# A mixer with a two-level mixture of experts: group places counted one tile later, counts on GpSimd, and other PSUM banks for the sums, the turns and the first down products

## The chip, the cores and the metric

The kernel runs on one core of one Trainium2 chip. The metric is the time of one launch on the device in microseconds; of several runs the median is taken. The engines of the core are named as the profile names them: PE (matmuls; PEld is its weight load), DVE (VectorE), ACT (ScalarE), POOL (GpSimd) and SP (SyncE, which here only issues DMAs). Matmuls write to PSUM, which has eight banks of 512 f32 columns; PE reads its operands from SBUF.

## What is computed

One layer on 1024 tokens of width 1024: a mixer (two kinds of gated linear attention), an output product, a norm, then 64 experts in 8 groups. Each token picks one group, and in it two experts; the experts' outputs are added with gates, and a second norm ends the layer.

```python
h = hybrid_mixer(x, w_in, w_a2, b_a, lb_all, norm_h, norm_g, w_out)
x = layer_norm(DEEPNORM_ALPHA * x + h, ln1_g, ln1_b)
# hierarchical_moe
p_group = softmax(xf @ w_group_router);  p_top_group, g_idx = top_k(p_group, 1)
e_logits = (xf @ w_expert_router)[the group's 8]
p_top, e_local = top_k(softmax(e_logits), 2)
gates = p_top_group * p_top / sum(p_top)
expert_id = g_idx * 8 + e_local
...
h = silu(xb @ w_gate[e]) * (xb @ w_up[e]);  yb = h @ w_down[e]
y = sum over a token's two experts of gate * yb
x = layer_norm(DEEPNORM_ALPHA * x + y, ln2_g, ln2_b)
```

## The kernel before

**Stages.** The mixer's projections and attention run first, to 421 us of the profile. Then comes the output product with the first norm and the router, tile by tile (a tile is 128 tokens, `NT` = 8 tiles). From about 562 us on the experts run in 32 pairs (`pairs`). The weights of all 64 experts, 402 MB, go through SBUF once, in 192 units of 2 MB: per pair two gate units, two up units, two down units. A few units are loaded ahead into the pools `w1` and `w2` (four buffers each) and two single buffers `w3u`. Every later unit takes the buffer of an earlier one, so SP issues its load only when PE has done the last product that reads the earlier one (`load_after`, `load_unit`, L793 and L800). SP issues its loads in program order.

**Router (`router`, L818 on).** For each tile DVE finds the group and the two experts from the logits `lg`, makes the one-hot rows `oh12` and from them `m`, 80 columns: 64 for the experts and 16 (`NE:NM`) for the groups, of which each is split into two classes, c = 0 and 1. A token's places among those of its expert and of its group and class are counts of the tokens ahead of it. `msum` is the running sum of `m` over the tiles before, and `msb` its copy in bf16.

**Places (`ranks`, L871 on).** For tile t two bf16 products add up in one bank `R` (tile name `lp`): `oneb` by `msb` gives the counts of all tiles before (L878), `trib` by `m` those of the tokens ahead in the tile (L879). DVE then reads `R` (`jk`, with the rank as its sum: L908 for the experts, L893 for the group), makes the one-hot `so` and `soc` of the ranks, and `tables` (L930) adds products of them into the bank `tabp`, from which come, for every slot of an expert, token number and gate (`tokf`, `gcol`) and, for every row of a group, its token (`rtok`, `gidx`). The pool of `lp` has one bank, and the logits of most tiles (L1024) use it too.

**Order.** In the loop over the tiles (L1089 on) tile t's output product `w_out`, its norm `norm1`, the places of tile t - 2, and the logits and router of tile t - 1 stand side by side; the order on each engine is set by the tile framework's scheduler, but for a few orders written by hand. In the last tile the places of tiles 6 and 7 follow each other, the table's part for the first expert pair (`sidx`) goes first, and then the rows of the first pair are gathered from `x1d` in DRAM (L1162).

**PSUM at the change of stages.** In the router stage `ps_h` (name `hp`) has banks 0 to 3, `ps_xt` 4 and 5, `ps_l` 6, `ps_t` (`tabp`) 7. In the experts' stage `ps_g` (`gu`) has 0 and 1, `ps_x` (`tp`, turns of x) 2 and 3, `ps_c` (`cp`, the sums) 4 to 7.

**Pairs (L1364 on).** First eight spreads bring the norms' constants, lying along partitions, to all rows (`spread`, L1353, four products of 128 columns each, which a DVE copy L1355 takes to SBUF): two in `gu` banks, four in `cp` banks ahead of pair 0, two in `cp` banks behind its up products. Then for each pair: the gate products (L1404, u = 0) and up products (u = 2) of two experts, 64 rows each; silu on ACT (L1410), the product with the up half on DVE (L1417); the turn of the next pair's rows (L1185 from the gathered rows for pairs 0 and 1; later L1191, products with a 0/1 matrix `pick` out of the group's rows, which `split_rows` has split in three bf16 `parts`); the turn of the hidden rows (L1207); the down products (L1361) into two banks `yps`; and their scaling into `y` by ACT (L1215) and DVE (L1216). The outputs of pair p - 1 are added to the group's rows by products with `adds` between the gate and up products of pair p (`add_rows`, L1322). For pair 0 the scaling comes behind both down products (L1452), since `y` lies where the last weights of pair 0 were. PE's order within `pairs` is the program's; that of the other engines is the scheduler's. The splitting of group 0's rows (L1294 to L1297, pair 1 in the program) is on ACT and DVE, that of later groups on ACT and GpSimd.

Of the kernel before, what the change touches and what calls it, by code (L numbers as in the profile page):

```python
# [10 lines left out]
F32 = mybir.dt.float32  # L11
# [10 lines left out]
NT = T // 128  # L22
# [37 lines left out]
def mixer_moe_kernel(ctx: ExitStack, tc: tile.TileContext, x_in, xT_in, wf_in, wv_in, wvg_in, wa2_in,  # L60
# [757 lines left out]
    def router(t):  # L818
# [18 lines left out]
        m = sp2.tile([128, NM], BF, name="m", bufs=3)  # L837
        msb = sp2.tile([128, NM], BF, name="msb", bufs=3)
        V.tensor_copy(msb, msum)
# [4 lines left out]
        V.scalar_tensor_tensor(mc_[:, :, 0], og, 0.0, mc_[:, :, 1], op0=OP.is_equal, op1=OP.subtract)  # L844
        count = lambda: V.tensor_tensor(msum, msum, m, OP.add)
# [24 lines left out]

    def ranks(t, E=V):  # L871

        m, msb = mt.pop(t)
        R = ps_l.tile([128, NM], F32, name="lp")
        own = t == NT - 1

        def counts(cs):
            PE.matmul(R[:, cs], oneb, msb[:, cs], start=True, stop=False)  # L878
            PE.matmul(R[:, cs], trib, m[:, cs], start=False, stop=True)  # L879
# [5 lines left out]
        def row_of():  # L885

            rhc = sp2.tile([128, 2 * NG], F32, name="rhc", bufs=1)
            if own:
                counts(slice(NE, NM))
            G.tensor_tensor(rhc, m[:, NE:NM], number.to_broadcast([128, 2 * NG]), OP.mult)  # L890
            jk = sp2.tile([128, NE], BF, name="jk")
            rc = sp2.tile([128, 1], F32, name="rc")
            o = V.scalar_tensor_tensor(jk[:, 0:2 * NG], m[:, NE:NM], 1.0, R[:, NE:NM], op0=OP.mult, op1=OP.mult,  # L893
                                       accum_out=rc)
            soc = sp2.tile([128, 128], F32, name="soc", bufs=1)
            V.tensor_tensor(soc, rowrank, rc.to_broadcast([128, 128]), OP.is_equal)
            rowst[t] = soc, rhc
            return o
# [19 lines left out]
        if own:  # L918
            return row_of
        row_of()  # L920
# [9 lines left out]
    def tables(t):  # L930

        so, rhs = rst.pop(t)
        row = PE.matmul(tabp[:, NE:NM], *rowst.pop(t), start=(t == 0), stop=False)
        for j in range(2):
            for b in range(2):
                o = PE.matmul(tabp[64 * b:64 * b + 64, 0:NE], so[:, j], rhs[:, j, b].rearrange("p k a -> p (k a)"),
                              start=False, stop=False)
                order(o, row, "the first product opens the bank")
# [112 lines left out]
    slots = sp2.tile([128, CAP], F32, name="slots", bufs=1)  # L1051
# [3 lines left out]
    expert = sp2.tile([128, NE], F32, name="expert", bufs=1)  # L1055
# [64 lines left out]
    for i, o in enumerate(ranks(t - 1, G)):  # L1120
# [10 lines left out]
    order(row_of(), first, "the rows that are to be fetched go first")  # L1131
# [6 lines left out]
    PE.matmul(gt[:, 32:32 + 2 * NG], *rowst.pop(t), start=True, stop=True)  # L1138
# [12 lines left out]
    ps_g = mp.enter_context(tc.tile_pool(name="ps_g", bufs=2, space=PSUM))  # L1151
    ps_x = mp.enter_context(tc.tile_pool(name="ps_x", bufs=2, space=PSUM))
    ps_c = mp.enter_context(tc.tile_pool(name="ps_c", bufs=4, space=PSUM))
# [58 lines left out]
    def scaled(yps, n, gate_col, yh, yl):  # L1212
# [3 lines left out]
        V.scalar_tensor_tensor(yl[:, ns], yps[n], gate_col, yh[:, ns], op0=OP.mult, op1=OP.subtract)  # L1216
# [72 lines left out]
    def split_rows(g, c, E):  # L1289
# [5 lines left out]
        E.tensor_tensor(rest, x, b0, OP.subtract)  # L1295
# [68 lines left out]
    def pairs():  # L1364

        nonlocal ring, home, parts
# [4 lines left out]
        for p in range(npair):  # L1371
# [54 lines left out]
            yps = [ps_g.tile([128, 512], F32, name="gu") for _ in range(2)]  # L1426
# [244 lines left out]
```

## Time and profile before

| | before |
|---|---|
| median of 3 runs | 1517.71 us (1516.21 to 1518.36) |
| the profiled execution | 1518.87 us, of which the span is 1517.1 |
| PE busy | 1443.5 us (95%) |
| DVE / ACT / POOL busy | 620.6 / 489.2 / 225.8 us (41 / 32 / 15%) |
| moved by DMA | 445.48 MB, mean 294 GB/s over the span |
| mean granted clock of PE | 0.990 |

The shares are means over stages with different limits: the mixer moves little (18 to 50 GB/s in most of its slices), the experts' stage moves 427 to 430 GB/s in most of its slices while PE is also 90% busy or more. The chain of waits that ended last has only two pieces, both at the very end on POOL, and says nothing of the rest. So the tables by stage and the timeline are what to read. One execution was profiled, and PE's half clock comes and goes in stretches of it; the granted clock stands in each row of the tables by stage.

### The profile page before, as it was taken

How to read it: one execution, taken by the hardware profiler on the slowest of the kernel's cores; microseconds unless marked ns; L12 is line 12 of the kernel's file. 1: busy time of each engine (PE TensorE's matmuls, PEld its weight loads, DVE VectorE, ACT ScalarE, POOL GpSimd, SP SyncE). 2: the span in 40 equal slices, each digit the busy share in tenths (PEclk: the TensorE clock that was granted, in tenths of full speed). 3: DMA queues.
4: the chain of work that ended last, by engine and by line, in shares of the span. 5: the costliest groups of instructions: out<-in, count | busy, mean ns of one | idle time of the engine just before them, and what ended most of it. 6: DMA issues, size and time to landing. Idle time of an engine off the chain costs nothing. (4 is left out here: it accounts for less than half of the span.)

```text
span 1517.1 us, 24694 instructions
## 1 busy us (share of the span) xinstructions
PE 1443.5 (95%) x10365; PEld 841.9 (55%) x10365; DVE 620.6 (41%) x1446; ACT 489.2 (32%) x961; POOL 225.8 (15%) x172
## 2 busy tenths in 40 slices
PE   9999999999999898999999999999999999999996
PEld 7888788887888773433433443444444344444432
DVE  6786673948545864142132132033033124114113
ACT  6656554457423323221321221222222221231120
POOL 0000001000012212140140140130130131032000
PEclk9999999999999979999999999999999999999999
DMA  5111111101284257999999999999999999999994
GB/s 182 50 36 43 30 43 29 41 18 45 91 346 168 112 197 279 416 429 428 429 429 427 430 429 427 429 430 426 428 429 427 429 430 427 429 429 427 427 424 202
DMA packets 58292, 445.48 MB, mean 294 GB/s; under 512 B 8916, under 2 KB 17364, under 8 KB 32576
## 3 DMA queue, kind: packets, MB, share of 16 engines
q1 hardware_dynamic: 51184, 430.00, 68.4%
q0 software_dynamic: 4896, 8.84, 1.6%
q10 hardware_dynamic: 2096, 5.01, 0.9%
q8 instruction: 82, 1.34, 0.4%
q14 instruction: 34, 0.28, 0.1%
HBM read 440.24 MB, written 12.58 MB: 298 GB/s over the span
## 5 line engine op out<-in xcount | busy, mean ns | idle before, releaser
L1404 PE MATMUL gu<-w1u,VOA 128*64 128x512 f32 x1024 | 248.1, 598 | 12.1 <-DMA w1u<-in_wu_dram 7.9
L1404 PE MATMUL gu<-w2u,VOA 128*64 128x512 f32 x992 | 239.3, 599 | 8.0 <-DVE y L1216 4.2
L1179 ACT ACTIVATE VOA<-tp,cols 128x128 f32<-128x128 f32 x256 | 96.2, 457 | 353.0 <-PE tp L1191 328.2
L1404 PEld LDWEIGHTS gu<-w1u,VOA 128*64 128x64 f32 x1024 | 83.3, 138 | 166.3 <-issue 131.1
L1404 PEld LDWEIGHTS gu<-w2u,VOA 128*64 128x64 f32 x992 | 88.0, 137 | 145.2 <-issue 108.4
L170 PE MATMUL pp<-xl,wh 128*128 128x512 f32 x416 | 164.8, 396 | 0.0
L170 PE MATMUL pp<-xh,wh 128*128 128x512 f32 x416 | 163.5, 393 | 0.6 <-ACT vt L223 0.6
L170 PE MATMUL pp<-xh,wl 128*128 128x512 f32 x416 | 163.2, 392 | 0.0
L1216 DVE SCALAR_TENSOR_TENSOR y<-gu,gcol,y 128x512 fp32r<-128x512 f32 x62 | 46.4, 750 | 242.7 <-ACT y L1215 242.5
L1361 PE MATMUL gu<-w2u,hT 128*64 128x512 f32 x512 | 117.4, 597 | 12.4 <-ACT VOA L1179 11.6
L1361 PE MATMUL gu<-w1u,hT 128*64 128x512 f32 x480 | 111.1, 598 | 13.4 <-ACT VOA L1179 12.5
L1191 PEld LDWEIGHTS <-parts 128*128 128x128 bf16 x1248 | 69.9, 98 | 48.8 <-issue 48.8
L1215 ACT ACTIVATE y<-gu,gcol 128x512 fp32r<-128x512 f32 x62 | 42.4, 686 | 142.8 <-PE gu L1361 142.8
L1417 DVE TENSOR_TENSOR sg<-sg,gu 128x512 f32<-128x512 f32 x32 | 22.0, 687 | 162.1 <-PE gu L1404 162.1
L170 PEld LDWEIGHTS pp<-xh,wh 128*128 128x128 f32 x416 | 78.1, 188 | 18.0 <-ACT vt L223 1.0
L170 PEld LDWEIGHTS pp<-xl,wh 128*128 128x128 f32 x416 | 78.1, 188 | 16.1 <-issue 0.2
L170 PEld LDWEIGHTS pp<-xh,wl 128*128 128x128 f32 x416 | 78.2, 188 | 15.5
L1410 ACT ACTIVATE sg<-gu 128x512 f32<-128x512 f32 x31 | 18.6, 599 | 195.0 <-PE gu L1404 195.0
L1191 PE MATMUL tp<-pick,parts 128*128 128x128 bf16 x1248 | 80.1, 220 | 0.8 <-DVE hT L1209 0.8
L1361 PEld LDWEIGHTS gu<-w2u,hT 128*64 128x64 f32 x512 | 40.8, 136 | 71.6 <-issue 51.1
L1361 PEld LDWEIGHTS gu<-w1u,hT 128*64 128x64 f32 x480 | 37.7, 136 | 64.8 <-issue 45.6
L1311 DVE TENSOR_SCALAR adds<-grow,tokf 128x256 fp32r<-128x256 f32 x31 | 19.0, 614 | 115.8 <-PE cp L1322 115.8
(343 smaller groups left out, 1961.7 us busy)
## 6 DMA issues: line engine op xcount, KB each, us to landing
w1u<-in_wg_dram SPq DMA_DIRECT2D x30, 2048.0 KB, 25.8
w1u<-in_wu_dram SPq DMA_DIRECT2D x30, 2048.0 KB, 29.0
w2u<-in_wg_dram SPq DMA_DIRECT2D x30, 2048.0 KB, 27.2
w2u<-in_wu_dram SPq DMA_DIRECT2D x30, 2048.0 KB, 29.8
w1u<-in_wd_dram SPq DMA_DIRECT2D x30, 2048.0 KB, 29.2
w2u<-in_wd_dram SPq DMA_DIRECT2D x28, 2048.0 KB, 27.8
wr<-in_wf_dram SPq DMA_DIRECT2D x36, 256.0 KB, 2.8
w1u<-in_wg_dram SPq DMA_DIRECT2D x8, 1024.0 KB, 21.4
```

The costliest lines, as they stand in the source:

```text
L170: PE.matmul(ps, w[:, k], x_[:, k, ts], start=(k == 0 and j == 0), stop=(k == KT - 1 and j == len(terms) - 1))
L1179: S.activation(xt[:, c], tp[:, i], AF.Identity, bias=cols[:, 42 + c:43 + c], scale=cols[:, 34 + c:35 + c])
L1191: PE.matmul(o, part[:, c], m, start=(i == 0), stop=(i == len(ms) - 1))
L1215: S.mul(yh[:, ns], yps[n], gate_col)
L1216: V.scalar_tensor_tensor(yl[:, ns], yps[n], gate_col, yh[:, ns], op0=OP.mult, op1=OP.subtract)
L1311: V.tensor_scalar(m, grow[0], tokf[:, p:p + 1], None, op0=OP.is_equal)
L1361: PE.matmul(yps[n][64 * b:64 * b + 64], hT[:, c, 64 * b:64 * b + 64], utile[6 * p + 4 + b][:, c, n * 512:(n + 1) * 512], start=(c == 0), s ...
L1404: PE.matmul(dst[64 * b:64 * b + 64], xt[:, c, 64 * b:64 * b + 64], utile[6 * p + u + b][:, c], start=(c == 0), stop=(c == KT - 1))
L1410: silu = S.activation(sg, gp, AF.Silu)
L1417: V.tensor_tensor(sg, sg, up, OP.mult)
```

## The change

It has these parts.

1. *Counts on GpSimd.* The copy `msb` and the running add into `msum` move from DVE to GpSimd (but for the last tile's add).
2. *Group places one tile later.* `R` of tile t holds the expert counts of tile t (64 columns) and the group counts of tile t - 1 (16 columns), as separate products. `row_of` becomes a function of its own, and makes the group row of tile t - 1; the last tile's group counts get a bank of their own, `lastR`, from `ps_h`. The first product that opens the bank `tabp` is now one of the expert products, without an order by hand.
3. *Types and forms.* `slots` and `expert` are bf16 instead of f32, and one `scalar_tensor_tensor` becomes a `tensor_tensor` with the same result on 0 and 1.
4. *Banks.* `ps_c` is opened ahead of `ps_x`: `cp` has banks 2 to 5, `tp` 6 and 7.
5. *The first pair's down products* go into two `cp` banks instead of the `gu` banks, and the subtractions that split group 0's rows stand behind the scaling of pair 0's outputs on DVE.

```diff
@@ router
-        m = sp2.tile([128, NM], BF, name="m", bufs=3)
-        msb = sp2.tile([128, NM], BF, name="msb", bufs=3)
-        V.tensor_copy(msb, msum)
+        m = sp2.tile([128, NM], BF, name="m", bufs=4)
+        msb = sp2.tile([128, NM], BF, name="msb", bufs=4)
+        G.tensor_copy(msb, msum)
...
-        V.scalar_tensor_tensor(mc_[:, :, 0], og, 0.0, mc_[:, :, 1], op0=OP.is_equal, op1=OP.subtract)
-        count = lambda: V.tensor_tensor(msum, msum, m, OP.add)
+        V.tensor_tensor(mc_[:, :, 0], og, mc_[:, :, 1], OP.is_equal)
+        count = lambda: (V if t == NT - 1 else G).tensor_tensor(msum, msum, m, OP.add)
@@ row_of, now outside ranks
+    def row_of(t, R):
+        m = mt.pop(t)[0]
+        rhc = sp2.tile([128, 2 * NG], F32, name="rhc", bufs=2)
+        G.tensor_tensor(rhc, m[:, NE:NM], cst[:, C_TOK + t:C_TOK + t + 1].to_broadcast([128, 2 * NG]), OP.mult)
...
+        o = V.scalar_tensor_tensor(jk[:, 0:2 * NG], m[:, NE:NM], 1.0, R[:, NE:NM], op0=OP.mult, op1=OP.mult,
+                                   accum_out=rc)
+        soc = sp2.tile([128, 128], F32, name="soc", bufs=1)
+        V.tensor_tensor(soc, rowrank, rc.to_broadcast([128, 128]), OP.is_equal)
+        rowst[t] = soc, rhc
+        return [o]
@@ ranks
-        def counts(cs):
-            PE.matmul(R[:, cs], oneb, msb[:, cs], start=True, stop=False)
-            PE.matmul(R[:, cs], trib, m[:, cs], start=False, stop=True)
-
-        counts(slice(0, NE if own else NM))
+        sums = [(k, u, cs, w_) for u, cs in ((t, slice(0, NE)), (t - 1, slice(NE, NM))) if u >= 0
+                for k, w_ in ((1, oneb), (0, trib))]
+        for i, (k, u, cs, w_) in enumerate(sums):
+            PE.matmul(R[:, cs], w_, mt[u][k][:, cs], start=(i == 0), stop=(i == len(sums) - 1))
...
-        if own:
-            return row_of
-        row_of()
+        if t:
+            ops += row_of(t - 1, R)
@@ tables
-        row = PE.matmul(tabp[:, NE:NM], *rowst.pop(t), start=(t == 0), stop=False)
...
+                PE.matmul(tabp[64 * b:64 * b + 64, 0:NE], so[:, j], rhs[:, j, b].rearrange("p k a -> p (k a)"),
+                          start=(t == 0 and j == 0), stop=False)
+        if t:
+            PE.matmul(tabp[:, NE:NM], *rowst.pop(t - 1), start=False, stop=False)
@@ behind the loop over the tiles
-    slots = sp2.tile([128, CAP], F32, name="slots", bufs=1)
+    slots = sp2.tile([128, CAP], BF, name="slots", bufs=1)
-    expert = sp2.tile([128, NE], F32, name="expert", bufs=1)
+    expert = sp2.tile([128, NE], BF, name="expert", bufs=1)
...
-    row_of = ranks(t)
+    late = ranks(t)[2:]
...
-    order(row_of(), first, "the rows that are to be fetched go first")
+    lastR = ps_h.tile([128, 512], F32, name="hp")
+    for k, w_ in ((1, oneb), (0, trib)):
+        PE.matmul(lastR[:, NE:NM], w_, mt[t][k][:, NE:NM], start=(k == 1), stop=(k == 0))
+    for o in late + row_of(t, lastR):
+        order(o, first, "the rows that are to be fetched go first")
...
-    PE.matmul(gt[:, 32:32 + 2 * NG], *rowst.pop(t), start=True, stop=True)
+    for u in (t - 1, t):
+        PE.matmul(gt[:, 32:32 + 2 * NG], *rowst.pop(u), start=(u < t), stop=(u == t))
@@ pools of the experts' stage
-    ps_x = mp.enter_context(tc.tile_pool(name="ps_x", bufs=2, space=PSUM))
     ps_c = mp.enter_context(tc.tile_pool(name="ps_c", bufs=4, space=PSUM))
+    ps_x = mp.enter_context(tc.tile_pool(name="ps_x", bufs=2, space=PSUM))
@@ split_rows
-        E.tensor_tensor(rest, x, b0, OP.subtract)
+        o = E.tensor_tensor(rest, x, b0, OP.subtract)
+        if g == 0:
+            order(o, evacuated, "the sums of the pair before go first")
@@ pairs
-            yps = [ps_g.tile([128, 512], F32, name="gu") for _ in range(2)]
+            yps = [ps_g.tile([128, 512], F32, name="gu") if p else ps_c.tile([128, 512], F32, name="cp") for _ in range(2)]
...
-                    scaled(yps, n, gcol[:, p:p + 1], ys[p][:, 0], ys[p][:, 1])
+                    evacuated = scaled(yps, n, gcol[:, p:p + 1], ys[p][:, 0], ys[p][:, 1])
```

The program order shows three places at which instructions stand elsewhere. A row is the line, the operation, and what is written from what.

The first is PE at the end of the router, behind the tables of tile 6 (`tabp`, with L928 before and L923 now as the last tile's first table product; `gu` and `cp` with L1353 or L1355 are the spreads). Before:

```order
L1353 MATMUL gu<-cst,cols 128x128 x8
L879 LDWEIGHTS trib
L879 MATMUL lp<-m,trib 128x64
L878 LDWEIGHTS oneb
L878 MATMUL lp<-msb,oneb 128x16
L879 LDWEIGHTS trib
L879 MATMUL lp<-m,trib 128x16
L928 MATMUL tabp<-rhs,so 64x32 x4
L928 MATMUL lp<-rhs,so 64x32 x4
L1138 MATMUL lp<-rhc,soc 128x16
L1353 MATMUL cp<-cst,cols 128x128 x16
L1185 MATMUL tp<-cst,VOA 128x128 x8
```

Now, from the last tile's own group product on:

```order
L1128 MATMUL hp<-m,trib 128x16
L923 MATMUL tabp<-rhs,so 64x32 x4
L1355 MATMUL gu<-cst,cols 128x128 x5
L923 MATMUL lp<-rhs,so 64x32 x4
L1138 MATMUL lp<-rhc,soc 128x16
L1355 MATMUL gu<-cst,cols 128x128 x2
L1138 MATMUL lp<-rhc,soc 128x16
L1355 MATMUL gu<-cst,cols 128x128
L1355 MATMUL cp<-cst,cols 128x128 x16
L1185 MATMUL tp<-cst,VOA 128x128 x8
```

The eight spread products in `gu` banks have moved from ahead of the last tile's counts to behind its first table product; those in `cp` banks stay behind the tables.

The second is DVE between the down products of pair 0 and the sums of pair 1 (`rest` and `parts` split group 0's rows; `y` is the scaling, `adds` the matrix for the sums). Before:

```order
L1304 TENSOR_SCALAR pick<-trow,rtok 128x128 x3
L1295 TENSOR_TENSOR rest<-VOA,parts 128x1024
L1216 SCALAR_TENSOR_TENSOR y<-gu,gcol,y 128x512 x2
L1311 TENSOR_SCALAR adds<-grow,tokf 128x256
L1297 TENSOR_TENSOR parts<-rest,parts 128x1024
L1295 TENSOR_TENSOR rest<-VOA,parts 128x1024
L1297 TENSOR_TENSOR parts<-rest,parts 128x1024
```

Now:

```order
L1306 TENSOR_SCALAR pick<-trow,rtok 128x128 x3
L1216 SCALAR_TENSOR_TENSOR y<-cp,gcol,y 128x512 x2
L1313 TENSOR_SCALAR adds<-grow,tokf 128x256
L1295 TENSOR_TENSOR rest<-VOA,parts 128x1024
L1299 TENSOR_TENSOR parts<-rest,parts 128x1024
L1295 TENSOR_TENSOR rest<-VOA,parts 128x1024
L1299 TENSOR_TENSOR parts<-rest,parts 128x1024
```

The scaling and `adds` have moved ahead of the first subtraction.

The third is PE in a tile of the router loop, between two output products (`hp`). Before:

```order
L956 MATMUL hp<-w2u,ol 128x512
L878 LDWEIGHTS oneb
L878 MATMUL lp<-msb,oneb 128x80
L1016 MATMUL xtp<-cst,w3u 128x128 x8
L879 LDWEIGHTS trib
L879 MATMUL lp<-m,trib 128x80
L954 MATMUL hp<-w2u,oh 128x512
```

Now:

```order
L951 MATMUL hp<-w2u,ol 128x512
L892 LDWEIGHTS oneb
L892 MATMUL lp<-msb,oneb 128x64
L892 LDWEIGHTS trib
L892 MATMUL lp<-m,trib 128x64
L892 LDWEIGHTS oneb
L892 MATMUL lp<-msb,oneb 128x16
L892 LDWEIGHTS trib
L892 MATMUL lp<-m,trib 128x16
L1011 MATMUL xtp<-cst,w3u 128x128 x8
L949 MATMUL hp<-w2u,oh 128x512
```

Two products of 80 columns have become four, of 64 and 16, and the turns (`xtp`), which stood between the two, now stand behind all four.

More of the change, by code (lines that the diff above doesn't have):

```diff
@@ L869, in router @@
         return gates
+    def row_of(t, R):
+        m = mt.pop(t)[0]
+        rhc = sp2.tile([128, 2 * NG], F32, name="rhc", bufs=2)
+        G.tensor_tensor(rhc, m[:, NE:NM], cst[:, C_TOK + t:C_TOK + t + 1].to_broadcast([128, 2 * NG]), OP.mult)
+        jk = sp2.tile([128, NE], BF, name="jk")
+        rc = sp2.tile([128, 1], F32, name="rc")
+        o = V.scalar_tensor_tensor(jk[:, 0:2 * NG], m[:, NE:NM], 1.0, R[:, NE:NM], op0=OP.mult, op1=OP.mult,
[4 more added lines that the diff above has]
+        return [o]
     def ranks(t, E=V):
-        m, msb = mt.pop(t)
         R = ps_l.tile([128, NM], F32, name="lp")
         own = t == NT - 1
-        def counts(cs):
-            PE.matmul(R[:, cs], oneb, msb[:, cs], start=True, stop=False)
-            PE.matmul(R[:, cs], trib, m[:, cs], start=False, stop=True)
-        counts(slice(0, NE if own else NM))
+        sums = [(k, u, cs, w_) for u, cs in ((t, slice(0, NE)), (t - 1, slice(NE, NM))) if u >= 0
+                for k, w_ in ((1, oneb), (0, trib))]
+        for i, (k, u, cs, w_) in enumerate(sums):
+            PE.matmul(R[:, cs], w_, mt[u][k][:, cs], start=(i == 0), stop=(i == len(sums) - 1))
         number = cst[:, C_TOK + t:C_TOK + t + 1]
         tokens = lambda: E.tensor_tensor(rhs[:, :, :, 0], ov, number[:, None, None, :].to_broadcast([128, 2, 2, 32]), OP.mult)
-        def row_of():
-            rhc = sp2.tile([128, 2 * NG], F32, name="rhc", bufs=1)
-            if own:
[L889 to L898, printed above, removed]
         rhs = sp2.tile([128, 2, 2, 2, 32], F32, name="rhs", bufs=1)
@@ L917, in ranks @@
         rst[t] = so, rhs
-        if own:
-            return row_of
-        row_of()
+        if t:
+            ops += row_of(t - 1, R)
         return ops
@@ L932, in tables @@
         so, rhs = rst.pop(t)
-        row = PE.matmul(tabp[:, NE:NM], *rowst.pop(t), start=(t == 0), stop=False)
         for j in range(2):
             for b in range(2):
-                o = PE.matmul(tabp[64 * b:64 * b + 64, 0:NE], so[:, j], rhs[:, j, b].rearrange("p k a -> p (k a)"),
-                              start=False, stop=False)
-                order(o, row, "the first product opens the bank")
+                PE.matmul(tabp[64 * b:64 * b + 64, 0:NE], so[:, j], rhs[:, j, b].rearrange("p k a -> p (k a)"),
+                          start=(t == 0 and j == 0), stop=False)
+        if t:
+            PE.matmul(tabp[:, NE:NM], *rowst.pop(t - 1), start=False, stop=False)
     hpt, mt, lgt, rtop, rst, rowst = {}, {}, {}, {}, {}, {}
@@ L1119, in mixer_moe_kernel @@
     gates = router(t)
-    for i, o in enumerate(ranks(t - 1, G)):
+    for i, o in enumerate(ranks(t - 1, G)[:2]):
         order(o, newton[-6 + 2 * i], "between the steps of the last tile's norm")
@@ L1215, in scaled @@
         S.mul(yh[:, ns], yps[n], gate_col)
-        V.scalar_tensor_tensor(yl[:, ns], yps[n], gate_col, yh[:, ns], op0=OP.mult, op1=OP.subtract)
+        return V.scalar_tensor_tensor(yl[:, ns], yps[n], gate_col, yh[:, ns], op0=OP.mult, op1=OP.subtract)
     def norm2(o, stats_of, w, root=None):
@@ L1364, in pairs @@
     def pairs():
-        nonlocal ring, home, parts
+        nonlocal ring, home, parts, evacuated
         last = npair - 1
@@ L1476, in pairs @@
         finish_rows(NG - 1, 1)
-    ring = home = parts = None
+    ring = home = parts = evacuated = None
     with tc.manual_schedule(engines={mybir.EngineType.PE}):
```

2 lines of the change are left out of this document (1 added, 1 removed).

## The prediction

> **What bounds the kernel now.** I read the page first, then a table by stage, then the issues of SyncE's queue. In the table a row gives the stretch, its length, the busy time of PE, PEld, DVE, ACT and POOL, the granted clock, the busy share of the DMA engines and GB/s.
>
> ```profile
> 592.00:594.00 2.00, 0.00 (x0) 0.00 (x0) 2.00 (x2) 1.37 (x4) 0.00 (x0) 1.00 0.53 156
> 594.00:604.00 10.00, 9.59 (x36) 3.35 (x37) 6.84 (x6) 4.50 (x4) 4.99 (x2) 0.83 0.01 3
> 606.00:640.00 34.00, 33.17 (x193) 13.72 (x190) 4.58 (x7) 7.89 (x13) 8.17 (x4) 1.00 0.99 413
> 900.00:1000.00 100.00, 93.96 (x498) 40.37 (x494) 20.24 (x43) 24.37 (x45) 11.09 (x7) 1.00 1.01 428
> ```
>
> From 606 us on the DMA engines are full, at 413 to 428 GB/s. Just before, from about 593 to 605, they stand empty (0.01). The weights are one stream whose next load waits until PE has used up a buffer, as the issues of SyncE show (start, length, what):
>
> ```profile
> 577.09 0.80 SPq L793 DMA_DIRECT2D w1u<-in_wg_dram  x2
> 603.22 0.80 SPq L793 DMA_DIRECT2D w2u<-in_wu_dram  x2
> 630.64 1.07 SPq L793 DMA_DIRECT2D w1u<-in_wu_dram  x2
> 657.96 0.80 SPq L793 DMA_DIRECT2D w1u<-in_wu_dram  x2
> L1410 ACT ACTIVATE sg<-gu x31: 597/599/601, 570.3 to 1457.2; 128x512 f32<-128x512 f32 x31
> ```
>
> After 577.09 nothing is issued until the gate products of pair 1 release two buffers at 603.22. From there PE alone would need 27.4 us a pair (603.22, 630.64, 657.96). But L1410 runs once a pair, and from pair 0 to pair 30 it takes (1457.2 - 570.3)/30 = 29.6 us. A pair has 12.6 MB, which is 29.4 us at 428 GB/s. So behind 603 DMA is the bound, PE has 2 us of slack a pair, and **the time of the kernel is the moment at which the stream resumes, plus a constant**. What moves the issue at 603.22 moves the end by as much, so long as it doesn't fall before the engines have drained (593). Every part of the change is judged by that.
>
> **Part 1, the seam between pairs 0 and 1.** Start, length, engine and line, what, and the idle time ahead with its releaser:
>
> ```profile
> 589.53 0.70 PE L1269 MATMUL tp<-sg,one 128*128 128x256 f32 x2
> 589.63 2.04 ACT L1294 CAST parts<-VOA 128x1024 bf16<-128x1024 f32 x1 [2.40 <-PE gu L1361]
> 591.58 1.26 ACT L1215 ACTIVATE y<-gu,gcol 128x512 fp32r<-128x512 f32 x2
> 591.71 1.99 DVE L1295 TENSOR_TENSOR rest<-VOA,parts 128x1024 f32<-128x1024 f32 x1 [3.75 <-ACT parts L1294]
> 593.62 1.39 DVE L1216 SCALAR_TENSOR_TENSOR y<-gu,gcol,y 128x512 fp32r<-128x512 f32 x2
> 594.41 8.78 PE L1404 MATMUL gu<-w2u,VOA 128*64 128x512 f32 x32 [4.18 <-DVE y L1216]
> 594.94 0.34 DVE L1311 TENSOR_SCALAR adds<-grow,tokf 128x256 fp32r<-128x256 f32 x1
> 600.03 2.41 DVE L1297 TENSOR_TENSOR parts<-rest,parts 128x1024 bf16<-128x1024 f32 x1 [1.11 <-ACT parts L1296]
> 603.13 2.11 PE L1322 MATMUL cp<-y,adds 128*128 128x512 f32 x8
> 605.17 7.09 PE L1404 MATMUL gu<-w2u,VOA 128*64 128x512 f32 x32
> 612.19 1.51 PE L1191 MATMUL tp<-pick,parts 128*128 128x128 bf16 x24
> 595.20:598.50 3.30, 3.30 (x10) 0.98 (x8) 2.80 (x3) 1.68 (x1) 0.00 (x0) 0.50 0.00 0
> ```
>
> The gate products of pair 1 want the two banks that hold pair 0's down products; these are emptied late, since DVE does `rest` first. With the down products in the sums' banks the 4.18 us wait has no reason left: PE goes on from L1269 at 590.2. The last row is the price that follows the wait: behind it the clock is granted at 0.50 for 3.3 us, so the 32 products take 8.72 us (594.41 to 603.13) against 7.02 for the same 32 at full clock (605.17 to 612.19). Without both they end at 590.2 + 7.0 = 597.2: **5.9 us** earlier. Bounds: -4.2 (the half clock stays) and -6.2 (L1269 is overlapped too).
>
> What is late next: the sums of pair 0 (L1322) now come at 597.2. They need `y` and `adds`. With `rest` behind them these start when ACT's first half of `y` is there (591.58 + 0.63 = 592.2), so 592.2 + 1.39 + 0.34 = 594.0, which is 3 us early. `rest` then starts at 594.0 instead of 591.71, and what follows it up to the last `parts` moves back by at most those 2.3 us: 602.44 becomes 604.7. The picks that read `parts` come at 612.19 - 5.9 = 606.3; 1.6 us are left.
>
> **Part 2, the spreads ahead of pair 0.** The sums' banks now stand where the router's turn banks stood, so that the spreads (L1353, bias columns through PE) need not wait for the tables to be read. The rows of before:
>
> ```profile
> 549.03 2.05 PE L1353 MATMUL gu<-cst,cols 128*128 128x128 f32 x16
> 552.21 0.42 PE L928 MATMUL tabp<-rhs,so 128*64 128x32 f32 x8 [0.17 <-DVE so L913]
> 554.20 0.64 PE L928 MATMUL lp<-rhs,so 128*64 128x32 f32 x8 [1.56 <-DVE rhs L1134]
> 554.77 0.61 PE L1138 MATMUL lp<-rhc,soc 128*128 128x16 f32 x2
> 555.83 6.29 PE L1353 MATMUL cp<-cst,cols 128*128 128x128 f32 x32 [0.45 <-DVE rtok L1143]
> 561.96 1.04 PE L1185 MATMUL tp<-cst,VOA 128*128 128x128 f32 x8
> 554.20:561.00 6.80, 6.35 (x34) 6.21 (x35) 4.53 (x11) 0.00 (x0) 3.20 (x3) 0.50 0.52 135
> 558.17 0.33 SPq L793 DMA_DIRECT2D w3u<-in_wd_dram  x1
> ```
>
> The wait on rtok is only 0.45 us. In the new order the first 16 records have left their place at 549 and stand behind the first table product (it ends at 552.63), mixed with the table products, and 32 follow. So 48 records and 1.25 us of tables come behind 552.63. A record takes 2.05/16 = 0.128 us at full clock and 6.13/32 = 0.19 at half. All at half gives 552.63 + 9.1 + 1.25 = 563.0, all at full 560.0; before it is 561.96. Before, full clock came back 5.2 us after dense spreads began (555.83 to 561.0). With the same delay from 552.63 on, 20 records run at half and 28 at full, ending at 561.4: **-0.6 us** (bounds +1.1 and -1.9). (The Trainium skill, "TensorE: Matmul & The Clock Gate", section "What's actually happening", has a rule against this move: a window of about 3.4 us with PE idle halves the clock, and only a busy window restores it. The half clock for 3.3 us behind the wait of 4.18 above agrees. PE, without the 16 records, is nearly idle from 549 to 552; by the rule the half rate can last up to two windows, 6.8 us, behind 552.63, and the term would be about 0.) The first gather of rows landed by 558.17, when the load that waits for it was issued, so it isn't what the turns wait for. Behind the tables DVE has a `jk` and a `soc` more to make (0.29, L896 below), for the last group product; the 16 records in front of it on PE cover that, and without them it costs those 0.3.
>
> **Part 3, the router's counts.** Rows of waits (total, times, longest) and of groups between 470 and 556 us (total, mean ns):
>
> ```profile
> PE lp L879 <- DVE m L844: 2.0, 3, 1.0
> PE lp L1024 <- DVE jk L893: 1.5, 1, 1.5
> L839 DVE CAST msb<-msum 128x80 bf16<-128x80 f32 x7 | 1.4, 193 | 0.0
> L845 DVE TENSOR_TENSOR msum<-msum,m 128x80 f32<-128x80 f32 x8 | 2.8, 351 | 0.0
> L844 DVE SCALAR_TENSOR_TENSOR m<-og,m 128x8 bf16<-128x8 f32 x8 | 3.1, 392 | 0.0
> L843 DVE TENSOR_TENSOR m<-m 128x8 bf16<-128x8 bf16 x8 | 1.3, 165 | 0.0
> L896 DVE TENSOR_TENSOR soc<-rowrank,rc 128x128 f32<-128x128 bf16 x8 | 2.3, 286 | 0.0
> L1031 POOL TENSOR_TENSOR lg<-lg,csb 128x72 f32<-128x72 f32 x7 | 2.2, 339 | 0.1
> L752 POOL TENSOR_TENSOR ol<-VOA,oh 128x512 fp32r<-128x512 f32 x6 | 7.7, 1277 | 22.8 <-PE xtp L1016 12.4 <-ACT oh L751 10.4
> L879 PE MATMUL lp<-m,trib 128*128 128x80 bf16 x7 | 1.5, 210 | 2.1 <-DVE m L844 2.0
> 530.30:540.50 10.20, 9.74 (x39) 8.46 (x38) 4.68 (x36) 2.43 (x7) 1.26 (x3) 0.50 0.18 66
> ```
>
> PE is in order, so the 2.0 us in which the trib product waited for the group columns of `m` go: these are now a tile old. Of the 1.5 us on jk I take half, 0.8, since DVE gets there with fewer instructions in front (3.8 us of casts and adds leave it, by 7 of each). Against that the 80 columns become 64 and 16, two more products a tile: at most 0.21 a pair by L879, over seven tiles 1.4 us. Sum: -2.0 - 0.8 + 1.4 = **-1.4 us**. GpSimd takes 14 small operations at about L1031's 0.34, 4.8 us in some 70; I cost them at nothing, hidden by the tile that lies between a count and its use. Gone that cover, each costs its tile 0.34 and what is ahead of it, L752's 1.28. The narrower types of `slots` and `expert` and the other form of L844: nothing, at most 0.1 a tile either way. Bounds: -7 us if also the half clock of 530 to 540 goes (9.74 us of work at half, 4.9 to win) and all of the 1.5, and +3.4 if no wait goes and 2 us of DVE stalls come (L844 takes 392 ns where its neighbour L843 takes 165: 1.8 us in eight).
>
> **Sum**: -5.9 - 0.6 - 1.4 = -7.9 us. The profiled execution took 1518.87 (span 1517.1 and 1.8 around it), which gives 1511.0; it lies 1.2 above the median of the runs, 1517.71, so my time is **1509.8**. The stream then resumes at 603.2 - 7.9 = 595.3, still behind the drain at 593, which itself comes about 2 us earlier with its gather: not capped.
>
> **Rivals.**
> - *The half clock at 530 goes too* (less PE waiting ahead of it speaks for it; that the stretch is short products in any case, against): some 3.7 us more, 1506.1. 15%.
> - *GpSimd stalls DVE.* L844 above, slow beside L752, speaks for it; that the new operations are short, against. Router +2.0 instead of -1.4: 1517.7 - 6.5 + 2.0 = 1513.2. 12%. (The Trainium skill, "SBUF — State Buffer", section "Who interferes with whom": a DVE instruction with two SBUF inputs and a GpSimd one that reads SBUF shut each other out for the whole instruction. The row of L844 agrees; by this rule the moved adds cost DVE part of what it saves.)
> - *The split of group 0 comes too late* for the picks: its 1.6 us of margin go if both `parts` run at 2.41 beside GpSimd and a cast is late. 1.5 us back: 1511.3. 7%.
> - *The stream doesn't wait for the seam*, or the freed wait returns at the sums: then only parts 2 and 3 are left, 1515.7. The share of 0.01 speaks against. 5%.
> - *Slower: GpSimd's queue holds PE.* The product with `msb` stands ahead of the turns on PE; `msb` stands behind L752 (1.28) and an add. If this comes out late in six tiles by 2 us each, 12 us are lost: 1517.7 - 6.5 + 12 = 1523.2. It is slower by over 3 us from 1.6 us a tile on. The tile of lead speaks against. 4%.
>
> The forecast itself: 57%. The range takes in the clock rival, the stalls and most of the bounds: 1504.5 to 1515.0. Faster by over 0.2% (3 us, about what a measurement of this kernel can tell from no change) 0.90, within it 0.06, slower 0.04.
>
> **What would show it.** Part 1: no PE wait on `y` ahead of pair 1's gate products, no half clock behind them, and 7.0 us for the 32 of them. Part 2: the spreads end, and the turns of pair 0 begin, 2 us earlier, near 560.0. Part 3: no PE wait on `m`, none on GpSimd, and L844 no slower than before. Sum: SyncE's issue behind pair 1's gate products comes at 595.3 instead of 603.2, and the last silu (1457.2) and the end as much earlier. I am wrong if the DMA engines are busy up to that issue, if PE waits at the picks of pair 2, or if it waits for `msb`.

## The result, and the profile after

| | before | after |
|---|---|---|
| median of 5 runs each, on one chip | 1518.36 us (1516.21 to 1520.65) | 1509.66 us (1506.55 to 1513.26) |
| ratio | | 0.9939, 95% interval 0.9918 to 0.9961 |
| profiled execution (span) | 1518.87 (1517.1) | 1513.26 (1511.4) |

The change saves 8.7 us; 7.9 were forecast, and a time of 1509.8. The profiled execution of after is the slowest of its five, so its end says little; its places are read against each other.

**The seam** came as forecast. PE of after between pairs 0 and 1 (start, length, what):

```profile
585.41 3.65 PE L1363 MATMUL cp<-w3u,hT 128*64 128x512 f32 x16
589.00 0.70 PE L1269 MATMUL tp<-sg,one 128*128 128x256 f32 x2
589.62 7.09 PE L1406 MATMUL gu<-w2u,VOA 128*64 128x512 f32 x32
596.64 2.12 PE L1324 MATMUL cp<-y,adds 128*128 128x512 f32 x8
598.69 7.09 PE L1406 MATMUL gu<-w2u,VOA 128*64 128x512 f32 x32
605.71 1.51 PE L1191 MATMUL tp<-pick,parts 128*128 128x128 bf16 x24
```

No wait stands ahead of the 32 gate products at 589.62 (before: 4.18 us on y), they take 7.0 us instead of 8.72, and the picks at 605.71 wait for nothing. SyncE's issues there (start, length, what), and then a table by stage (the columns as in the first table of the prediction):

```profile
576.60 0.80 SPq L793 DMA_DIRECT2D w1u<-in_wg_dram  x2
596.74 0.80 SPq L793 DMA_DIRECT2D w2u<-in_wu_dram  x2
605.80 0.81 SPq L793 DMA_DIRECT2D w2u<-in_wd_dram  x2
```

```profile
592.00:598.00 6.00, 6.00 (x28) 2.43 (x25) 4.66 (x6) 4.18 (x5) 0.00 (x0) 1.00 0.35 77
594.00:597.00 3.00, 3.00 (x16) 1.00 (x13) 1.70 (x2) 2.87 (x3) 0.00 (x0) 1.00 0.02 5
606.00:640.00 34.00, 32.27 (x199) 14.23 (x197) 5.10 (x8) 10.05 (x19) 9.30 (x4) 1.00 0.99 413
```

From 576.60 to 596.74 are 20.1 us, before 26.1 (577.09 to 603.22): 6.0 us, where 5.9 were forecast. The DMA engines are 0.35 busy from 592 to 598: they run dry, stand empty from 594 to 597 (0.02), start again with the issue, and are full from 606 on (0.99). From that issue to the end of the span are 913.9 us before, 914.7 after, and 912.1 to 914.4 in the nine profiles below that leave pairs 1 to 3 as they are, while the issue itself lies anywhere from 590.5 to 603.2. So the time is the moment of the resume plus a constant, as forecast, to within 2.6 us.

**The router and the spreads** did not come as forecast. PE of after in the last tile:

```profile
546.64 0.40 PE L933 MATMUL tabp<-rhc,soc 128*128 128x16 f32 x2
549.24 0.21 PE L892 MATMUL lp<-m,trib 128*128 128x64 bf16 x1 [2.20 <-DVE m L840]
...
549.89 0.17 PE L1128 MATMUL hp<-m,trib 128*128 128x16 bf16 x1 [0.40 <-DVE m L844]
550.39 0.64 PE L923 MATMUL tabp<-rhs,so 128*64 128x32 f32 x8 [0.33 <-DVE so L909]
551.76 2.48 PE L1355 MATMUL gu<-cst,cols 128*128 128x128 f32 x10 [0.73 <-DVE jk L878]
...
557.03 4.60 PE L1355 MATMUL cp<-cst,cols 128*128 128x128 f32 x32
561.47 1.04 PE L1185 MATMUL tp<-cst,VOA 128*128 128x128 f32 x8
```

From the end of the first table product (551.03) to the turns are 10.44 us; before they were 9.33 (552.63 to 561.96). The spreads, forecast at -0.6, cost 1.1. The second row is new: 2.20 us of PE with nothing to do. There the 16 gu records stood before (549.03 to 551.08). They now wait for the read of the last group counts (`jk`, L878), whose bank `lastR` lies where the gu banks will be. The clock of after in the stage from that gap on:

```profile
549.00:558.80 9.80, 8.10 (x49) 7.47 (x49) 5.42 (x32) 0.00 (x0) 2.42 (x3) 0.50 0.46 125
```

Half clock from 549 to 558.8; before it was 554.2 to 561. Against that, the router up to the last output product takes 76.43 us from one of SyncE's issues at the start of its stage (465.94 to 542.37), where it took 79.88 (464.37 to 544.25): 3.4 us less, where the forecast had 1.4. The two stretches, before and after, with one of a later run (`e_noorder`) that met no half clock there:

```profile
464.37:544.25 79.88, 74.82 (x430) 62.50 (x428) 55.91 (x290) 27.52 (x57) 17.32 (x31) 0.94 0.34 129
465.94:542.37 76.43, 74.50 (x438) 62.01 (x439) 54.05 (x273) 27.29 (x57) 20.54 (x44) 0.93 0.36 134
463.98:536.37 72.39, 70.40 (x438) 58.07 (x439) 54.08 (x273) 27.30 (x57) 20.65 (x44) 1.00 0.38 142
```

Before and after lose the same clock in it (0.94 and 0.93). PE sits idle for 5.1 us of the first and 1.9 of the second, and its busy time falls by 0.3.

### The profile page after: what moved, and what is told of

The parts are those of the page before. It is cut to its first block, busy times and chain, and to the rows that moved or that the text cites. A ratio compares the mean times of both kernels' runs of the same rounds, so it can differ in the third digit from the quotient of the medians.

```text
span 1511.4 us, 24708 instructions
## 1 busy us (share of the span) xinstructions
PE 1445.2 (96%) x10379; PEld 837.4 (55%) x10379; DVE 621.4 (41%) x1431; ACT 488.5 (32%) x961; POOL 228.6 (15%) x187
## 5 line engine op out<-in xcount | busy, mean ns | idle before, releaser
L1406 PEld LDWEIGHTS gu<-w2u,VOA 128*64 128x64 f32 x992 | 83.8, 137 | 149.1 <-issue 115.5
```

Source lines behind the costliest of these rows:

```text
L1406: PE.matmul(dst[64 * b:64 * b + 64], xt[:, c, 64 * b:64 * b + 64], utile[6 * p + u + b][:, c], start=(c == 0), stop=(c == KT - 1))
```

## The experiments

Eleven runs of ten kernels in three groups, each group on one chip with its own runs of the kernel before (medians 1517.78, 1518.71 and 1518.70). The second and third groups were on the same chip; kernels of different groups are compared by their ratios. The mean granted clock is that of all runs of a kernel.

| run | median us | ratio to before, 95% | mean clock |
|---|---|---|---|
| before (first group) | 1517.78 | | 0.9906 |
| after (first comparison) | 1509.66 | 0.9939 [0.9918, 0.9961] | 0.9912 |
| e_seam | 1512.20 | 0.9964 [0.9950, 0.9978] | 0.9915 |
| e_noseam | 1513.65 | 0.9976 [0.9967, 0.9984] | 0.9918 |
| e_noorder | 1508.25 | 0.9941 [0.9927, 0.9956] | 0.9927 |
| e_countsV | 1509.83 | 0.9942 [0.9929, 0.9955] | 0.9918 |
| e_xfirst | 1507.83 | 0.9929 [0.9917, 0.9940] | 0.9923 |
| f_lastxt | 1503.64 | 0.9901 [0.9883, 0.9918] | 0.9953 |
| f_lastxt_again | 1503.54 | 0.9897 [0.9879, 0.9916] | 0.9942 |
| e_fill | 1505.10 | 0.9923 [0.9903, 0.9943] | 0.9938 |
| f_xt_x | 1505.93 | 0.9920 [0.9904, 0.9937] | 0.9938 |
| f_release | 1542.59 | 1.0165 [1.0150, 1.0180] | 0.9926 |
| f_both | 1538.89 | 1.0131 [1.0116, 1.0145] | 0.9945 |

### The seam alone: e_seam

```diff
 (the kernel before; `o` is the first subtraction, `evacuated` the last scaling of pair 0, as in the change)
+        if g == 0:
+            order(o, evacuated, "the sums of the pair before go first")
...
-            yps = [ps_g.tile([128, 512], F32, name="gu") for _ in range(2)]
+            yps = [ps_g.tile([128, 512], F32, name="gu") if p else ps_c.tile([128, 512], F32, name="cp") for _ in range(2)]
```

> The kernel before with only the fifth part of the change: the first pair's down products in two cp banks, and the first subtraction of group 0's split behind the scaling of pair 0; router, counts and banks as before. Theory (the seam is worth what the change's own trace shows, 6.0 us, and the stream's resume moves the end one to one): no PE wait on y ahead of pair 1's gate products, SyncE's issue behind them 6.0 us earlier measured from the start of pair 0's gate products (40.1 becomes 34.1), and about 1512.2 us where the kernel before has 1518.2. Rival 1 (the router gives it all, DMA hides the seam): within 1 us of the kernel before. Rival 2 (part of the seam's gain needs the other banks or the lighter router): the issue comes 3 us earlier and the end as much.

Measured: 5.6 us faster. Pair 0's gate products start at 562.91 and the issue behind pair 1's comes at 597.02, 34.1 us later, as expected; no wait on y is left. So the seam is worth nearly all of its 6 us without the other parts. Rival 1 falls, and so does rival 2.

### Everything but the seam: e_noseam

```diff
 (the changed kernel)
-        if g == 0:
-            order(o, evacuated, "the sums of the pair before go first")
...
-            yps = [ps_g.tile([128, 512], F32, name="gu") if p else ps_c.tile([128, 512], F32, name="cp") for _ in range(2)]
+            yps = [ps_g.tile([128, 512], F32, name="gu") for _ in range(2)]
```

> The changed kernel without its fifth part: the first pair's down products in the gu banks again, and no order between the scaling and the split. Theory (router -3.4 as the change's trace shows, spreads +1.1, together -2.3): SyncE's issue behind pair 1's gate products 40 us behind the start of pair 0's gate products, as before, with the 4 us wait on y and the half clock back, and about 1516 us. My own forecast of the two terms was -1.4 and -0.6, which gives 1516.2: the sum can't tell the two, but the trace does: last output product to the first table product, and that to the turns of pair 0 (before 9.33 us, after 10.44). Rival (the seam is worth less than 6 because the stream is held elsewhere): 1512 or less.

Measured: 4.1 us faster than before, twice what either sum expected. Its waits have the old seam back:

```profile
PE gu L1404 <- DVE y L1216: 4.2, 1, 4.2
PE lp L892 <- DVE m L840: 2.4, 2, 2.2
```

The spreads are as in after (first table product's end 545.57, turns 556.51: 10.9 us). So the router itself must have won more than 4 us. Its stages show how (from 530 us on, and behind the gap):

```profile
530.00:540.00 10.00, 9.89 (x68) 8.13 (x68) 8.92 (x53) 3.51 (x9) 2.73 (x10) 1.00 0.48 161
544.40:554.50 10.10, 9.02 (x51) 8.46 (x51) 5.68 (x28) 0.00 (x0) 2.43 (x3) 0.50 0.48 143
```

In this execution nothing is left of the half clock of 530 to 540 (1.00; 0.50 in before); of the router's half clock only that behind the gap remains. The profile of after has it in part:

```profile
530.00:540.00 10.00, 9.53 (x45) 8.43 (x44) 5.83 (x40) 3.56 (x10) 2.29 (x6) 0.66 0.28 106
```

Both have the same router. So one profile of it can have this stretch at half clock and the next not. Of the eleven profiles with the new router, seven meet no half clock up to the last output product and take 72.4 us from SyncE's issue; e_countsV meets 3.4 us of it and takes 74.5; after, f_lastxt and f_lastxt_again meet 10.2 us and take 76.4 to 76.5. The two with the old router (before, e_seam) meet 10.2 us and take 79.8 to 79.9. So at equal clock the new router is worth 3.4 us, and this half clock another 4.0 where it stays away.

### Without the order on DVE: e_noorder

```diff
 (the changed kernel)
-        if g == 0:
-            order(o, evacuated, "the sums of the pair before go first")
```

> The changed kernel with the down products in the cp banks, but without the order that puts the first subtraction of the split behind the scaling: DVE does rest first again, so y and adds come about 2 us later. Theory (only the banks matter, since pair 1's gate products no longer want the banks that y is read from, and y at 594 plus 2 still is ahead of the sums at 596.7): no wait on y, the same time as the changed kernel within 0.7 us. Rival (the order is half of the seam's gain): PE waits 1 to 2 us at the sums (L1322 here), 1 to 2 us slower.

Measured: 1508.25, with 1509.66 for the changed kernel (ratios 0.9941 and 0.9939); no loss. DVE does `rest` first again, at 584.96, `adds` ends at 588.56, and the sums begin at 590.42 without a wait. The banks alone do the work.

### Counts on DVE again: e_countsV

```diff
-        G.tensor_copy(msb, msum)
+        V.tensor_copy(msb, msum)
...
-        count = lambda: (V if t == NT - 1 else G).tensor_tensor(msum, msum, m, OP.add)
+        count = lambda: V.tensor_tensor(msum, msum, m, OP.add)
```

> The changed kernel with the casts of msb and the adds into msum on DVE again. Theory (the router's gain comes from the group columns that are read a tile later, since PE no longer waits for m; what GpSimd takes is off the path): within 1 us of the changed kernel, no PE wait on m in the tiles but the last, DVE 3.8 us busier between 470 and 556. Rival 1 (the lighter DVE is half of the gain, by the 0.8 us that I took for it or more): 1 to 2 us slower, PE waits on jk and m come back. Rival 2 (GpSimd's adds shut DVE out of SBUF): 1 us faster, and L844 at 0.39 us or less.

Measured: 1509.83, the same as the changed kernel within the noise. No PE wait on m comes back but the last tile's. One wait grows:

```profile
PE lp L892 <- DVE m L840: 2.4, 2, 2.3
PE tabp L930 <- DVE so L909: 2.0, 3, 1.0
```

The second row was 0.9 in after: 1.1 us of PE, which the end doesn't show. Who counts is off the path. That the waits on `m` go with the counts on either engine fits the group columns' being read a tile later; no run has that delay alone. L844 takes 301 ns in the mean with the counts on either engine (392 before), and the mean hides two kinds of it. In after:

```profile
505.65 1.29 POOL L752 TENSOR_TENSOR ol<-VOA,oh 128x512 fp32r<-128x512 f32 x1 [3.86 <-ACT oh L751]
505.73 1.24 DVE L844 TENSOR_TENSOR m<-og,m 128x8 bf16<-128x8 f32 x1
515.92 0.17 DVE L844 TENSOR_TENSOR m<-og,m 128x8 bf16<-128x8 f32 x1
517.28 1.29 POOL L752 TENSOR_TENSOR ol<-VOA,oh 128x512 fp32r<-128x512 f32 x1 [0.35 <-ACT oh L751]
```

Where it starts inside GpSimd's L752 it ends only with it; elsewhere it takes 0.17 us, in the old form too. Before, two of its eight fall inside (1.23 us at 505.46 and 0.97 at 515.71), now one. So the shorter mean comes neither from the new form nor from the counts' engine but from where L752 falls.

### The banks in the old order: e_xfirst

```diff
-    ps_c = mp.enter_context(tc.tile_pool(name="ps_c", bufs=4, space=PSUM))
     ps_x = mp.enter_context(tc.tile_pool(name="ps_x", bufs=2, space=PSUM))
+    ps_c = mp.enter_context(tc.tile_pool(name="ps_c", bufs=4, space=PSUM))
```

> The changed kernel with the banks in the old order: tp in 2 and 3, cp in 4 to 7, so that the last cp spreads write to the banks of the tables. The order of the instructions is that of the changed kernel. Theory (the order of the banks is worth little: the cp spreads stand behind the tables anyway, and before they waited 0.45 us for the last read): 0.3 to 0.7 us slower, a PE wait on rtok ahead of a cp spread. Rival (the order of the banks is what lets PE go on into the turns): 2 us slower, the turns of pair 0 more than 12 us behind the last tile's first table product, instead of 10.4. Rival 2 (it costs): faster, as the turns wait for nothing in banks 2 and 3.

Measured: 1507.83, and no wait on rtok ahead of the spreads; the turns come 11.0 us behind the first table product (544.34 to 555.33). Against e_countsV on the same chip it is 2.0 us faster with overlapping intervals. As the change stands, no worth of the order of the banks could be measured.

### The last group counts in another bank: f_lastxt, f_lastxt_again

```diff
-    lastR = ps_h.tile([128, 512], F32, name="hp")
+    lastR = ps_xt.tile([128, 4, 128], F32, name="xtp").rearrange("p a b -> p (a b)")
```

> The changed kernel with one edit: the bank of the last tile's group counts comes from ps_xt (a bank that becomes a cp bank) instead of ps_h (one that becomes a gu bank). Theory (the spreads lost 1.1 us instead of winning 0.6 because the gu banks stay taken by the last group counts until DVE has read them, so that PE stands idle ahead of the last tile's counts where the 8 spreads stood before): the 8 gu spreads go ahead of the last tile's counts again and 8 of the cp spreads go among the tables; PE's wait of 2.2 us on m in the last tile holds work again, the turns of pair 0 begin 1.1 to 2.2 us earlier measured from the last output product, and the end as much. Rival (the half clock behind the idle time is the cause, and it stays, as the stretch is short products): the order changes but the turns come within 0.5 us of the changed kernel's. Rival 2 (the rows of the first pair are the limit): no change, PE waits for the gather.

Measured: 1503.64, 14.1 us under the kernel before and 4.6 under e_noorder on the same chip, with intervals that don't overlap. PE of f_lastxt in the last tile:

```profile
546.92 0.40 PE L933 MATMUL tabp<-rhc,soc 128*128 128x16 f32 x2
547.43 2.05 PE L1355 MATMUL gu<-cst,cols 128*128 128x128 f32 x16
549.50 0.19 PE L892 MATMUL lp<-m,trib 128*128 128x64 bf16 x1
...
550.60 0.43 PE L923 MATMUL tabp<-rhs,so 128*64 128x32 f32 x8 [0.43 <-DVE so L909]
551.75 1.96 PE L1355 MATMUL cp<-cst,cols 128*128 128x128 f32 x10 [0.72 <-DVE jk L878]
...
555.95 3.77 PE L1355 MATMUL cp<-cst,cols 128*128 128x128 f32 x18
559.55 1.04 PE L1185 MATMUL tp<-cst,VOA 128*128 128x128 f32 x8
```

The gap holds the gu spreads again, 14 of the 32 cp records have gone among the tables, and the turns come 8.5 us behind the first table product (551.03 to 559.55), 1.9 earlier than in after. From SyncE's issue at the start of the router's stage to the turns are 93.36 us (466.19 to 559.55), with 95.53 in after (465.94 to 561.47), and both have 10.2 us of half clock in the router: 2.2 us. That is the 1.1 to 2.2 expected; the rest of the 4.6 is not in this trace. Its six executions point to the clock: at 0.991 it took 1509.0, at 0.994 and 0.995 1505.1 and 1505.0, at 0.996 1502.3, at 0.998 1501.1 and 1499.0.

> The same kernel as the earlier run with the last group counts in a bank of ps_xt, again, for more executions and a second profile beside the filled gap. If the clock carries the gain: the executions with the highest mean clock (0.998) are the fastest, some 9 us under those with 0.991, as 0.007 of 1505 us is 10.5, and the median is 1503 to 1505. If the first five were luck: 1506 to 1508.

Measured: 1503.54, from 1501.5 at 0.996 to 1507.4 at 0.991. The first median was not luck. Both profiled executions are the slowest of their runs (1509.0 and 1507.4, 0.991); none at 0.994 or more was profiled, so where those lost their half clock stays open.

### Useless work in the gap: e_fill

```diff
 (the changed kernel; logits_end is the last tile's last logit product)
+    idle = ps_xt.tile([128, 4, 128], F32, name="xtp")
+    for k in range(8):
+        o = PE.matmul(idle[:, k % 4], cols[:, 34 + k:35 + k].to_broadcast([128, 128]), ident, start=True, stop=True)
+        order(o, logits_end, "in the gap ahead of the last counts")
```

> The changed kernel with 8 useless products (16 records, 128 columns each, as a spread's) put on PE into the gap ahead of the last tile's counts, written to a bank of ps_xt that nobody reads; nothing else is moved, the spreads stay behind the tables. It parts two reasons why the bank edit won 4.6 us. Theory 1 (the clock: PE idle for 2.2 us there lowers the granted clock to 0.50 in the windows that follow, 10.2 us in every profile with the gap): the wait of 2.2 us on m is filled, less than 10.2 us of half clock follow, the mean clock of the runs rises from 0.992 toward 0.995, and the time comes 2 to 3 us under the changed kernel's 1508 to 1509.7. Theory 2 (the work: 2.05 us of spreads have left the path, and the clock is what it was): same clock, same time as the changed kernel or up to 0.5 us slower. Both may hold, then 1 to 2 us.

Measured: 1505.10, with 16 records more for PE to do. By the ratios that is 0.0018 or 2.7 us under e_noorder and 0.0006 or 0.9 us under e_xfirst, which both have the hole; the intervals overlap, so the times alone don't show a gain. PE of e_fill, and its stages behind the gap:

```profile
542.67 0.91 PE L1124 MATMUL xtp<-cst,cols 128*128 128x128 f32 x6
543.77 0.19 PE L892 MATMUL lp<-m,trib 128*128 128x64 bf16 x1 [0.19 <-DVE m L840]
...
546.05 2.32 PE L1359 MATMUL gu<-cst,cols 128*128 128x128 f32 x10 [0.72 <-DVE jk L878]
```

```profile
542.40:546.00 3.60, 2.00 (x24) 1.45 (x20) 2.84 (x21) 0.60 (x4) 0.22 (x1) 1.00 0.40 150
546.40:553.00 6.60, 6.60 (x37) 6.31 (x36) 3.31 (x14) 0.00 (x0) 2.21 (x2) 0.50 0.45 112
553.00:556.00 3.00, 3.00 (x29) 3.00 (x29) 2.91 (x7) 0.00 (x0) 0.99 (x1) 0.99 0.98 415
```

The spreads stand where they stood in after, and the turns come 10.3 us behind the first table product (545.33 to 555.64), but the wait on m is 0.19 instead of 2.20 and the half clock behind lasts 6.8 us instead of 10.2. The other profiles bear this out: the six with the hole all have 10.2 us there, the seven without it 6.8. So the hole does lengthen the half clock behind it, as theory 1 had it.

It is worth less than the medians say. From SyncE's issue at the start of the router's stage to the turns are 91.15 us in e_fill (464.49 to 555.64). The four profiles with the hole that met no half clock in the router either take 91.28, 91.55, 91.99 and 92.00 (e_noorder, f_release, e_noseam, e_xfirst), so the filling is worth 0.1 to 0.9 us there. The mean clock of the runs rises to 0.9938, but the router's half clock, which comes and goes, moves it as well; that the rest of the 2.7 us is the hole's is not shown. (The Trainium skill, "TensorE: Matmul & The Clock Gate", section "What's actually happening", has the clock halved after at least one idle window of some 3.4 us, and says that the windows run freely and do not restart with the kernel. The stretches here are multiples of 3.4 us, which agrees; but no single wait of PE ahead of them was that long: 2.20 us in after, 0.72 in e_fill.)

### The gap filled, the banks in the old order: f_xt_x

Both edits, that of f_lastxt and that of e_xfirst.

> The last group counts in a bank of ps_xt, and the banks in the old order (tp in 2 and 3, cp in 4 to 7): the gu spreads go into the gap, all 16 cp spreads stand behind the tables, as in the kernel before. Theory (now that the gap is filled, the order of the banks is worth what the 7 cp spreads among the tables fill, 0.72 us on jk and the rest of PE's waits there): the turns of pair 0 about 9.3 us behind the last tile's first table product, as before, instead of 8.5, and 1 to 2 us slower than with the banks of the change. Rival (the order of the banks is worth nothing at all): the same within 0.5 us.

Measured: 1505.93, 2.4 us slower than f_lastxt_again on the same chip, with overlapping intervals. The turns come 10.1 us behind the first table product (546.72 to 556.78) instead of 8.5, since all 32 cp records stand behind the tables:

```profile
548.40 0.42 PE L923 MATMUL lp<-rhs,so 128*64 128x32 f32 x8 [1.68 <-DVE rhs L1133]
...
550.77 6.17 PE L1355 MATMUL cp<-cst,cols 128*128 128x128 f32 x32 [0.45 <-DVE rtok L1143]
```

By the trace the order of the banks is worth some 1.5 us once `lastR` is out of the way: f_both (below), with the banks of the change and its other edit behind the turns, takes 89.36 us from SyncE's issue to the turns (465.90 to 555.26), f_xt_x 90.89 (465.89 to 556.78), and neither met half clock in the router. The times agree in sign, within their noise.

### Releasing the weights one expert at a time: f_release, f_both

```diff
 (in essence, for pairs 1 to 3; the down products and their loads in the same manner)
-                for c in range(KT):
-                    for b in range(2):
-                        PE.matmul(dst[64 * b:64 * b + 64], xt[:, c, 64 * b:64 * b + 64], utile[6 * p + u + b][:, c],
-                                  start=(c == 0), stop=(c == KT - 1))
-                for b in range(2):
-                    load_after(6 * p + u + b)
+                for b in range(2):
+                    for c in range(KT):
+                        PE.matmul(dst[64 * b:64 * b + 64], xt[:, c, 64 * b:64 * b + 64], utile[6 * p + u + b][:, c],
+                                  start=(c == 0), stop=(c == KT - 1))
+                    load_after(6 * p + u + b)
```

> The changed kernel with another order of products in pairs 1 to 3: gate, up and down products of a pair's first expert ahead of those of the second (the same products, the same sums), and each weight unit's successor is loaded as soon as its own products are done. Theory (behind the seam the DMA stream sets the end, it has been empty from 593.5 to 596.7, and it needs 29.4 / 6 = 4.9 us a unit): SyncE's first issue behind the start of pair 1's gate products comes 3.5 us behind it instead of 7.1, the next one at 7.1, the DMA engines aren't empty between pair 0 and 2, and the end comes 3 to 4 us earlier than the changed kernel's: 1505 to 1506. Rival (the time is PE's from there on): PE does the same work, no gain, within 1 us of the changed kernel.

> The edits of the two runs before together: the last group counts in a bank of ps_xt, and the first expert's products first in pairs 1 to 3. Theory: the two gains add, since one moves pair 0's start and the other the resume of the stream behind it; 3 to 4 us under the run with the bank alone (1503.6), so 1500. Rival (what the spreads' place gained is the same stall of the stream that the early release takes away): no more than the better of the two alone, 1503.

Both were misses: 32.8 us slower than e_countsV on the same chip, and 29.1 for f_both. PE of f_release in pair 1, gate (but for its first two records), sums and up, and a stage behind:

```profile
585.44 11.38 PE L1406 MATMUL gu<-w2u,VOA 128*64 128x512 f32 x30
596.75 2.11 PE L1324 MATMUL cp<-y,adds 128*128 128x512 f32 x8
598.79 12.29 PE L1406 MATMUL gu<-w2u,VOA 128*64 128x512 f32 x32
```

```profile
640.00:700.00 60.00, 58.26 (x204) 22.05 (x204) 13.57 (x30) 9.82 (x18) 16.11 (x8) 1.00 0.83 315
```

The same 32 products take 12.29 us at full clock instead of 7.09. PE becomes the bound (58.3 of 60 us busy, DMA at 0.83), and whether an earlier release helps was not seen. f_both is 3.7 us faster than f_release, the bank edit's gain again, in another kernel. To the turns, with no half clock in either router, it is 2.2 us (91.55 to 89.36), as in f_lastxt.

## Why the prediction was right

**The bound and the seam: right, in mechanism and size.** Forecast -5.9; the profile of after has 6.0 between the issues, e_seam has 5.6 at the end. By an estimate (each run's time less (1 - its clock) x 1510 us, as if all lost clock lay on the path) the medians are 1503.3 before and 1499.4 for e_seam: 3.9 us are the wait of 4.18, and the rest is the half clock behind it. What the stream's resume gained came through to the end nearly whole, as the first part had it. The order on DVE, to which the working gave the margins, was not needed: e_noorder.

**The router: right in its sign, mis-sized.** The forecast term was -1.4: 2.8 us of waits less, and 1.4 more for two more products a tile. At equal clock the stage up to the last output product became 3.4 shorter. The waits were sized about right, as PE's idle time there fell by 3.1 us (5.1 to 1.9). The step that failed is the 1.4: PE's busy time didn't rise but fell by 0.3 (74.82 to 74.50). The rival that the half clock of 530 goes too, at 15% and 3.7 us, was not one case against another. It happens in seven of the eleven profiles with the new router, in one it goes in part, and in three 10.2 us of half clock stay in the router; it is worth 4.0 us. That fits e_noseam, in which router and spreads stand alone and which gained 4.1 where the two terms made 2.0.

**The spreads: wrong.** The step that failed is that the spreads "need not wait for the tables to be read", with a price of -0.6 for the 16 records that left their place. They left it because `lastR` sits in a future gu bank, and what they left was a hole of 2.20 us in front of the last counts. I noted that PE would be "nearly idle from 549 to 552" and priced it at next to nothing. The term came to +1.1 in the profile, the bound that I had worked out for half clock throughout. What the place of `lastR` cost in all: by the traces 2.2 us (f_lastxt against after, f_both against f_release), by the medians 4.6, of which the part beyond 2.2 goes with the runs' clock and stays open. Filling the hole with useless products gave back 0.1 to 0.9 us by the traces, 2.7 by medians that don't stand clear of the noise. The clock rule weighed there had put the term at 0, nearer to +1.1 than my value.

**The rivals.** The counts on GpSimd neither stalled DVE (of L844 only the one inside L752 is slow, with the counts on either engine) nor held PE (no wait for `msb`); L752 does stall DVE, before and after, as the rival had it. The split was not late; the stream did wait for the seam. The total came so near to the forecast by luck in part, since the error of the router's term (too small a gain) and that of the spreads' (a loss taken for a gain) have opposite signs.

The fastest kernel found is the changed one with `lastR` in a bank of `ps_xt`: 1503.6, a ratio of 0.9901 [0.9883, 0.9918].

## What to carry to other kernels

Where a DMA stream bounds what follows, look for the moment at which it resumes: what holds a buffer there is worth its full time (6.0 us at the issue, 5.6 at the end here). What lies behind can only lose while the stream is the bound: that follows from the reasoning, and f_release shows the losing side. When an edit moves work out of a gap on PE, price the gap too: the work comes back elsewhere, and the half clock behind the hole lasted 3.4 us longer in every profile that had it. A new PSUM tile at a change of stages holds up whoever takes its bank next, so choose its bank by who comes next.

## What the runs showed of the hardware

- Products that write 64 of the 128 rows of a bank go faster if they alternate between the two halves: 32 of them take 7.09 us alternating (after) and 12.29 us one half after the other (f_release), at full clock in both. The Trainium skill has matmuls at different tile positions of the array overlap ("TensorE: Matmul & The Clock Gate", section "The mechanism"); the 1.73 times between these two numbers agree.
- The half clock comes in stretches of 3.4, 6.8 or 10.2 us, and the same code meets them in one execution and not in the next. In six executions of f_lastxt the mean clock went from 0.991 to 0.998 and the time from 1509.0 to 1499.0 us. As 0.007 of 1505 us is 10.5, the clock accounts for about all of that spread (an estimate).
- A DVE operation of 128x8 that takes 0.17 us takes 0.97 to 1.24 us when it starts inside GpSimd's product of 128x512 (1.26 to 1.29 us), and ends with it (before, after and e_countsV).
